# Rotary embedding on one core: a one-row store between the first two loads, and one early row in place of two

## The chip, the cores and the metric

The kernel runs on one core of a Trainium2 chip. The metric is the device time of one execution in microseconds. Before the change the median of three runs is 316.54 us (316.42 to 316.58).

Four engines matter. VectorE (DVE in the profile) does all the arithmetic. ScalarE (ACT) converts between f32 and f16. GpSimd (POOL) issues nearly all transfers; SyncE (SP) issues three and ACT one. The transfers run on 16 DMA engines. TensorE is not used.

## The reference

`x` is [8, 2048, 16, 64] in f32 (batch, position, head, head dimension); `cos` and `sin` are [2048, 32]. Each head vector is cut in two halves of 32, which are rotated against each other by an angle of the position:

```python
cos = cos[None, :, None, :]
sin = sin[None, :, None, :]
out1 = x1 * cos - x2 * sin
out2 = x1 * sin + x2 * cos
return np.concatenate([out1, out2], axis=-1).astype(np.float32)
```

The input and the output are 67.1 MB each, in f32, and each element is read once and written once.

## The kernel before

**Tiles.** A batch has 2048 positions. Partition p of 128 holds J = 16 consecutive positions ("rows"), each of 16 x 64 = 1024 values; a batch is thus 16384 values a partition. The tile `buf` has five slots (`NBUF`), each for one batch, in f16; batch b is in slot b mod 5. Loads from `x` convert f32 to f16 on the way and stores to `out` convert f16 to f32. Both are issued on POOL's queue (lines 71 and 81). A full batch moves 65,536 bytes of f32 a partition on either way.

**Arithmetic.** `rotate` does three VectorE instructions for a range of rows of one batch: a product with the signed sine of the swapped halves into a temporary `v` (line 92), a product with the cosine in place (line 98), and their sum (line 100). ACT prepares the f16 tables `sin_h` and `cos_h` at the start (lines 104 to 106).

**The head rows.** The first JA = 2 rows of batch 0 come another way, so that VectorE can begin early: SyncE loads them as f32 into the tile `head` (line 42), behind the load of `sin` (line 41), and ACT copies them as f16 into slot 0 (line 107). `load(0)` then brings the other 14 rows (`j0 = JA` at line 65). `rotate(0, 0, JA)` works on these two rows alone. At the end of the kernel the same tile is used for the last two rows of batch 7: ACT converts them to f32 (line 134) and SyncE stores them (line 135), while POOL stores rows 0 to 8 and 9 to 13 of that batch.

**Order.** The order of the transfers is written out by hand. The helper `in_ring` (line 51) ties every transfer of POOL to the one before it, so POOL issues them in the order of the program: load 0, load 1, the store of row 0 of batch 0 (line 112), load 2 and 3 as one, load 4, the store of rows 1 to 15 of batch 0, the stores of batches 1 and 2, load 5 and 6, load 7, the stores of 3 and 4, of 5 and 6, and of 7 in its parts. POOL waits in that order too: while it waits for VectorE before a store, the transfers behind it in this list are not issued. Load 5 and 6 waits until the stores of batches 0 and 1 have landed, and load 7 for that of batch 2, since they reuse their slots.

Of the kernel before, what the change touches and what calls it, by code (L numbers as in the profile page):

```python
# [1 line left out]

# [4 lines left out]


@with_exitstack  # L10
def kernel(
    ctx: ExitStack,
    tc: tile.TileContext,
    x: bass.AP,
    cos: bass.AP,
    sin: bass.AP,
    out: bass.AP,
):
    nc = tc.nc
    f16 = mybir.dt.float16  # L20
    f32 = mybir.dt.float32

    B, S, H, D = x.shape
    Dh = D // 2
    P = nc.NUM_PARTITIONS
    J = S // P
    NBUF = 5

    const_pool = ctx.enter_context(tc.tile_pool(name="rope_const", bufs=1))
    io_pool = ctx.enter_context(tc.tile_pool(name="rope_io", bufs=1))  # L30
    tmp_pool = ctx.enter_context(tc.tile_pool(name="rope_tmp", bufs=1))

    JA = 2
    head = const_pool.tile([P, JA, H, D], f32)
    x0 = x[0].rearrange("(p j) h d -> p j (h d)", j=J)
    sin_f = const_pool.tile([P, J, Dh], f32)
    cos_f = const_pool.tile([P, J, Dh], f32)
    cos_h = const_pool.tile([P, J, Dh], f16)
    sin_h = const_pool.tile([P, J, D], f16)
    nc.scalar.dma_start(out=cos_f, in_=cos.rearrange("(p j) d -> p j d", j=J))  # L40
    nc.sync.dma_start(out=sin_f, in_=sin.rearrange("(p j) d -> p j d", j=J))
    nc.sync.dma_start(
        out=head.rearrange("p j h d -> p (j h d)"),
        in_=x0[:, 0:JA, :].rearrange("p j f -> p (j f)"),
    )

    buf = io_pool.tile([P, NBUF, J, H, D], f16)

    ring = []

    def in_ring(dma):
        if ring:
            tc.add_manual_dep(
                dma.ins,
                ring[-1].ins.name,
                mybir.DependencyInfo(mybir.DependencyClass.NoSync, mybir.DependencyReason.DATA),
                reason="order of the ring",
            )
        ring.append(dma)
        return dma  # L60

    def load(b, n=1):
        k = b % NBUF
        if n == 1:
            j0 = JA if b == 0 else 0
            dst = buf[:, k, j0:J, :, :].rearrange("p j h d -> p (j h d)")
            src = x[b].rearrange("(p j) h d -> p j (h d)", j=J)[:, j0:J, :].rearrange("p j f -> p (j f)")
        else:
            dst = buf[:, k : k + n, :, :, :].rearrange("p b j h d -> p b (j h d)")
            src = x[b : b + n].rearrange("b (p j) h d -> p b (j h d)", j=J)  # L70
        in_ring(nc.gpsimd.dma_start(out=dst, in_=src))  # L71

    def store(b, n=1, j0=0, j1=J):
        k = b % NBUF
        if n == 1:
            src = buf[:, k, j0:j1, :, :].rearrange("p j h d -> p (j h d)")
            dst = out[b].rearrange("(p j) h d -> p j (h d)", j=J)[:, j0:j1, :].rearrange("p j f -> p (j f)")
        else:
            src = buf[:, k : k + n, :, :, :].rearrange("p b j h d -> p b (j h d)")
            dst = out[b : b + n].rearrange("b (p j) h d -> p b (j h d)", j=J)  # L80
        return in_ring(nc.gpsimd.dma_start(out=dst, in_=src))  # L81

    def rotate(b, j0=0, j1=J):
        v = tmp_pool.tile([P, J, H, D], f16)
        n = j1 - j0
        js = slice(j0, j1)
        xt = buf[:, b % NBUF, js, :, :]
        shape = [P, n, H, 2, Dh]
        sin_b = sin_h[:, js, :].rearrange("p j (e d) -> p j e d", e=2).unsqueeze(2).to_broadcast(shape)
        cos_b = cos_h[:, js, :].unsqueeze(2).to_broadcast([P, n, 2 * H, Dh])  # L90
        xe = xt.rearrange("p j h (e d) -> p j h e d", e=2)
        nc.vector.tensor_mul(  # L92
            out=v[:, js, :, :].rearrange("p j h (e d) -> p j h e d", e=2),
            in0=xe[:, :, :, ::-1, :],
            in1=sin_b,
        )
        xw = xt.rearrange("p j h (e d) -> p j (h e) d", d=Dh)
        nc.vector.tensor_mul(out=xw, in0=xw, in1=cos_b)  # L98
        xa = xt.rearrange("p j h d -> p (j h d)")
        nc.vector.tensor_add(out=xa, in0=xa, in1=v[:, js, :, :].rearrange("p j h d -> p (j h d)"))  # L100

    load(0)
    load(1)
    nc.scalar.copy(out=sin_h[:, :, Dh:D], in_=sin_f)  # L104
    nc.scalar.mul(out=sin_h[:, :, 0:Dh], in_=sin_f, mul=-1.0)  # L105
    nc.scalar.copy(out=cos_h, in_=cos_f)  # L106
    nc.scalar.copy(  # L107
        out=buf[:, 0, 0:JA, :, :].rearrange("p j h d -> p (j h d)"),
        in_=head.rearrange("p j h d -> p (j h d)"),
    )  # L110
    rotate(0, 0, JA)
    store(0, 1, 0, 1)
    load(2, 2)
    load(4)
    rotate(0, JA, J)
    store(0, 1, 1, J)
    rotate(1)
    store(1)
    rotate(2)
    store(2)  # L120
    load(5, 2)
    load(7)
    rotate(3)
    rotate(4)
    store(3, 2)
    rotate(5)
    rotate(6)
    store(5, 2)
    rotate(7)
    gate = store(7, 1, 0, 9)  # L130
    store(7, 1, 9, J - JA)
    last = buf[:, 7 % NBUF, J - JA : J, :, :].rearrange("p j h d -> p (j h d)")
    dst = out[B - 1].rearrange("(p j) h d -> p j (h d)", j=J)[:, J - JA : J, :].rearrange("p j f -> p (j f)")
    nc.scalar.copy(out=head.rearrange("p j h d -> p (j h d)"), in_=last)  # L134
    end = nc.sync.dma_start(out=dst, in_=head.rearrange("p j h d -> p (j h d)"))
    tc.add_manual_dep(
        end.ins,
        gate.ins.name,
        mybir.DependencyInfo(mybir.DependencyClass.Sync, mybir.DependencyReason.DATA),
        reason="the last rows go out behind this part",  # L140
    )


# [1 line left out]
_INS = ['x', 'cos', 'sin']  # L145
_OUTS = [((8, 2048, 16, 64), 'float32')]


# [23 lines left out]
```

## Time and profile before

| what | value |
|---|---|
| median of three runs | 316.54 us |
| profiled execution, its own time | 316.39 us |
| its span, first to last instruction | 314.6 us |
| outside the span (316.39 - 314.6) | 1.8 us |
| VectorE busy | 209.1 us (66% of the span) |
| ACT busy, POOL busy | 6.7 us, 8.6 us |
| share of the 16 DMA engines taken by POOL's queue (q0) | 98.1% |
| by SP's (q1), by ACT's (q10) | 1.9%, 0.2% |
| HBM read and written | 67.63 MB, 67.11 MB |
| the two head rows, issue to landing | 12.0 us |
| load of the other 14 rows, issue to landing | 22.5 us |
| store of row 0, issue to landing | 25.3 us |

The busy time of an engine says how much it worked, not whether anybody waited for it. The share of the DMA engines is the time that their packets took, over 16 times the span. The trace also holds a record for each packet: its start, its length in time, its queue and its size on the receiving side. Here a packet is what one partition gets or gives in one transfer, and each DMA engine carries 8 of the 128.

### The profile page before, as it was taken

To read this page: it belongs to the slowest core of one execution; us is meant where nothing else is said; L and a number is where in the kernel's file an instruction comes from. 1 tells how busy PE (TensorE), PEld (TensorE's weight loads), DVE (VectorE), ACT (ScalarE), POOL (GpSimd) and SP (SyncE) were. 2 spreads that over 40 slices of the span, in tenths; PEclk is the share of its full clock that TensorE was granted. 3 is DMA by queue.
4 is the path that set the end of the run, shared out by engine and by line. 5 is a ranking of instruction groups with operands and counts; after the bars stand their busy time and mean duration, and the time that the engine had idled before them with its cause. 6 is when DMAs were issued, how large, how long until landed. Compare 5 with 4: busy or idle time off the path is not lost.

```text
span 314.6 us, 114 instructions
## 1 busy us (share of the span) xinstructions
DVE 209.1 (66%) x27; ACT 6.7 (2%) x6; POOL 8.6 (3%) x18
## 2 busy tenths in 40 slices
DVE  0039999992499999999950000899999999910000
ACT  3200000000000000000000000000000000020000
POOL 1020000000000000000010000000000000010000
DMA  7999999999999899999999999999999999999998
GB/s 240 252 242 200 200 267 200 200 267 200 200 200 325 375 500 400 400 400 533 400 200 221 246 200 200 246 221 333 400 508 425 400 400 525 408 400 400 433 425 342
DMA packets 3104, 101.71 MB, mean 323 GB/s; under 512 B 288, under 2 KB 288, under 8 KB 672
## 3 DMA queue, kind: packets, MB, share of 16 engines
q0 software_dynamic: 2528, 99.09, 98.1%
q1 hardware_dynamic: 432, 2.36, 1.9%
q10 hardware_dynamic: 144, 0.26, 0.2%
HBM read 67.63 MB, written 67.11 MB: 428 GB/s over the span
## 4 chain that ended last, share of the span: by engine, by line
DVE 65%; another core or an unknown queue 15%; DMA 7%; ACT 1%; issue 0%; DVEq 0%; ACTq 0%; PEldq 0%
DVE buf L98 22%; DVE v L92 22%; DVE buf L100 22%; DMA buf<-in_x_dram 7%; ACT head L134 1%; DVEq L92 0%; ACTq L134 0%; PEldq L167 0%
## 5 line engine op out<-in xcount | busy, mean ns | idle before, releaser
L92 DVE TENSOR_TENSOR v<-buf,sin_h 128x16384 f16<-128x16384 f16 (+2 forms) x9 | 69.7, 7744 | 66.6 <-DMA buf<-in_x_dram 51.3
L98 DVE TENSOR_TENSOR buf<-buf,cos_h 128x16384 f16<-128x16384 f16 (+2 forms) x9 | 69.7, 7744 | 0.3
L100 DVE TENSOR_TENSOR buf<-buf,v 128x16384 f16<-128x16384 f16 (+2 forms) x9 | 69.7, 7744 | 0.3
L81 POOL DMA_DIRECT2D out_dram<-buf x8 | 4.7, 584 | 219.2 <-DVE buf L100 219.2
L134 ACT CAST head<-buf 128x2048 f32<-128x2048 f16 x1 | 1.9, 1897 | 261.3 <-DVE buf L100 261.3
L71 POOL DMA_DIRECT2D buf<-in_x_dram x6 | 3.7, 628 | 49.7 <-DMA out_dram<-buf 48.9
L107 ACT CAST buf<-head 128x2048 f16<-128x2048 f32 x1 | 1.9, 1897 | 7.1 <-DMA head<-in_x_dram 7.1
L104 ACT ACT_TABLE_LOAD x1 | 1.3, 1283 | 1.2 <-PEq L156 1.2
L104 ACT CAST sin_h<-sin_f 128x512 f16<-128x512 f32 x1 | 0.6, 617 | 2.0 <-DMA sin_f<-in_sin_dram 2.0
L105 ACT ACTIVATE sin_h<-sin_f 128x512 f16<-128x512 f32 x1 | 0.6, 624 | 0.0
L106 ACT CAST cos_h<-cos_f 128x512 f16<-128x512 f32 x1 | 0.6, 601 | 0.0
L156 POOL MEMSET const-float32-0.0<- 128x1 f32 x1 | 0.1, 98 | 0.2 <-issue 0.2
L156 POOL MEMSET const-bfloat16-1.0<- 128x1 bf16 x1 | 0.1, 101 | 0.0
L156 POOL MEMSET const-uint8-127<- 128x1 uint8 x1 | 0.1, 99 | 0.0
L156 POOL MEMSET const-float32-1.0<- 128x1 f32 x1 | 0.1, 98 | 0.0
## 6 DMA issues: line engine op xcount, KB each, us to landing
buf<-in_x_dram POOLq DMA_DIRECT2D x2, 8192.0 KB, 60.3
buf<-in_x_dram POOLq DMA_DIRECT2D x3, 4096.0 KB, 57.4
out_dram<-buf POOLq DMA_DIRECT2D x1, 7680.0 KB, 73.5
out_dram<-buf POOLq DMA_DIRECT2D x1, 4608.0 KB, 28.6
buf<-in_x_dram POOLq DMA_DIRECT2D x1, 3584.0 KB, 22.5
out_dram<-buf POOLq DMA_DIRECT2D x1, 2560.0 KB, 34.1
head<-in_x_dram SPq DMA_DIRECT2D x1, 1024.0 KB, 12.0
out_dram<-head SPq DMA_DIRECT2D x1, 1024.0 KB, 8.4
```

Source lines behind the costliest of these rows:

```text
L71: in_ring(nc.gpsimd.dma_start(out=dst, in_=src))
L81: return in_ring(nc.gpsimd.dma_start(out=dst, in_=src))
L92: nc.vector.tensor_mul(out=v[:, js, :, :].rearrange("p j h (e d) -> p j h e d", e=2), in0=xe[:, :, :, ::-1, :], in1=sin_b,)
L98: nc.vector.tensor_mul(out=xw, in0=xw, in1=cos_b)
L100: nc.vector.tensor_add(out=xa, in0=xa, in1=v[:, js, :, :].rearrange("p j h d -> p (j h d)"))
L104: nc.scalar.copy(out=sin_h[:, :, Dh:D], in_=sin_f)
L105: nc.scalar.mul(out=sin_h[:, :, 0:Dh], in_=sin_f, mul=-1.0)
L106: nc.scalar.copy(out=cos_h, in_=cos_f)
L107: nc.scalar.copy(out=buf[:, 0, 0:JA, :, :].rearrange("p j h d -> p (j h d)"), in_=head.rearrange("p j h d -> p (j h d)"),)
L134: nc.scalar.copy(out=head.rearrange("p j h d -> p (j h d)"), in_=last)
L156: nc = _bacc.Bacc("TRN2", target_bir_lowering=False, num_devices=1)
```

## The change

Two edits. `JA` becomes 1: SyncE loads one row of batch 0 into `head`, ACT copies one row, the first `rotate` works on one row, and `load(0)` brings 15 rows in place of 14. The tile `head` keeps its size of two rows (`JE = 2`), and the end of the kernel still handles two rows through it. And `load(1)` moves from ahead of the first `rotate` to behind the store of row 0, so POOL's order begins: load 0, the store of row 0, load 1, load 2 and 3, load 4.

```diff
-    JA = 2
-    head = const_pool.tile([P, JA, H, D], f32)
+    JA = 1
+    JE = 2
+    head = const_pool.tile([P, JE, H, D], f32)
...
     nc.sync.dma_start(
-        out=head.rearrange("p j h d -> p (j h d)"),
+        out=head[:, 0:JA, :, :].rearrange("p j h d -> p (j h d)"),
         in_=x0[:, 0:JA, :].rearrange("p j f -> p (j f)"),
     )
...
     load(0)
-    load(1)
     nc.scalar.copy(out=sin_h[:, :, Dh:D], in_=sin_f)
...
     nc.scalar.copy(
         out=buf[:, 0, 0:JA, :, :].rearrange("p j h d -> p (j h d)"),
-        in_=head.rearrange("p j h d -> p (j h d)"),
+        in_=head[:, 0:JA, :, :].rearrange("p j h d -> p (j h d)"),
     )
     rotate(0, 0, JA)
     store(0, 1, 0, 1)
+    load(1)
     load(2, 2)
     load(4)
...
-    store(7, 1, 9, J - JA)
-    last = buf[:, 7 % NBUF, J - JA : J, :, :].rearrange("p j h d -> p (j h d)")
-    dst = out[B - 1].rearrange("(p j) h d -> p j (h d)", j=J)[:, J - JA : J, :].rearrange("p j f -> p (j f)")
+    store(7, 1, 9, J - JE)
+    last = buf[:, 7 % NBUF, J - JE : J, :, :].rearrange("p j h d -> p (j h d)")
+    dst = out[B - 1].rearrange("(p j) h d -> p j (h d)", j=J)[:, J - JE : J, :].rearrange("p j f -> p (j f)")
```

## The prediction

> **What bounds the kernel now.** I read the page first: busy shares, the DMA rows, the queues, the HBM line.
>
> ```profile
> DVE 209.1 (66%) x27; ACT 6.7 (2%) x6; POOL 8.6 (3%) x18
> ...
> DMA  7999999999999899999999999999999999999998
> ...
> q0 software_dynamic: 2528, 99.09, 98.1%
> q1 hardware_dynamic: 432, 2.36, 1.9%
> q10 hardware_dynamic: 144, 0.26, 0.2%
> HBM read 67.63 MB, written 67.11 MB: 428 GB/s over the span
> ```
>
> VectorE works two thirds of the span. The DMA row is at 9 in all slices but the first, one in the middle and the last, and the queues' shares add to just over 100%: the 16 DMA engines bound the kernel. The chain of waits names VectorE for 65%, but only because it follows what ended last; VectorE waits for loads three times, and the engines are full meanwhile. The packet records say how full. Added up by the microsecond, packets cover 0.67 of the 16 engines between 2 and 3 us, 1.00 or a little more in every stretch that I added up from 3 to 313 us, 0.44 from 313 to 314 and nothing after. (A packet is recorded as starting some 20 ns before the one ahead of it on its engine has ended.) So the time is: 2 to 3 us until the engines are full, 310 us of packets, 1 us to close. A change can move it by altering the packets' total, or by leaving engines without packets.
>
> Next the start, from the timeline, where both edits lie.
>
> ```profile
> 0.74 0.38 SPq L41 DMA_DIRECT2D sin_f<-in_sin_dram  x1
> 1.17 0.43 SPq L42 DMA_DIRECT2D head<-in_x_dram  x1
> 1.24 1.21 POOL L71 DMA_DIRECT2D buf<-in_x_dram  x2 [0.80 <-PEq L167]
> ...
> 5.51 0.60 ACT L106 CAST cos_h<-cos_f 128x512 f16<-128x512 f32 x1
> 13.22 1.90 ACT L107 CAST buf<-head 128x2048 f16<-128x2048 f32 x1 [7.11 <-DMA head<-in_x_dram]
> 15.15 1.23 DVE L92 TENSOR_TENSOR v<-buf,sin_h 128x2048 f16<-128x2048 f16 x1 [15.15 <-ACT buf L107]
> ...
> 19.19 0.54 POOL L81 DMA_DIRECT2D out_dram<-buf  x1 [16.74 <-DVE buf L100]
> 19.72 1.27 POOL L71 DMA_DIRECT2D buf<-in_x_dram  x2
> 23.87 7.63 DVE L92 TENSOR_TENSOR v<-buf,sin_h 128x14336 f16<-128x14336 f16 x1 [4.98 <-DMA buf<-in_x_dram]
> ```
>
> POOL issues load 0 at 1.24, but the first packet of its queue starts at 5.73. Until then the engines carry sin, cos and the head rows: the head's first packets start between 3.89 and 4.34 us by engine. From 5.73 on a head packet and a packet of load 0 take turns on each engine (2.13 us of load 0, then 0.32 of head, then load 0 again), so the head's last two packets wait for two long ones, and the head lands at 13.2.
>
> **The packets' total does not change.** On an engine a packet occupies, start to start, 0.306 us for 8,192 bytes of f32 (head), 0.153 for 4,096 (the row-0 store), 2.111 for 57,344 (load 0; recorded as 28,672 of f16) and 2.412 for 65,536: 26.8 to 27.2 bytes a nanosecond whatever the size. The head's 8 packets an engine shrink from 8 x 0.306 = 2.45 us to 8 x 0.153 = 1.22, less 1.22; load 0's 8 packets grow by 15/14 to 2.262 each, 8 x 0.151 = 1.21 more. Packet counts are as before. Sum: 0.0 us, within 0.02.
>
> **The row-0 store in another place.** It takes the same 8 packets an engine: after load 0 at about 24 us in place of after load 1 at 42.8. In the records of before, one engine's last load packet ends at 42.83, its eight store packets follow at 0.153 each, and load 2 starts at 44.07, with nothing left open on either side. A boundary of load and store before and one of store and load behind it are there in both orders: 0.0 us.
>
> **The added wait.** In the new order POOL waits for VectorE's row 0 before it issues load 1, and load 2 and 3 and load 4 behind that. Cover: load 0 keeps the engines busy to about 23.8 us. The head, one row, should have all its packets through by 4.34 + 8 x 0.153 = 5.56 us, on the latest engine, before load 0's first packets: it lands near 5.7. ACT is free at 6.1; its copy of 1024 values costs 1.04 us, between the rows 0.617 for 512 and 1.897 for 2048. The three VectorE instructions cost 0.69 each (1.225 for 2048 and 7.626 for 14336 give 0.521 ns a value and 0.16 fixed). 6.1 + 1.04 + 3 x 0.69 + 0.1 for gaps = 9.3; POOL's store at 9.6 (0.3 behind VectorE, as at 19.19 before), load 1 at 10.2, the rest by 12.1. From an issue to its first packet the only row is 1.24 to 5.73, 4.5 us, so the store can be ready at 14.1, and load 1 just behind: 9 us before they are needed. Cost 0; if that cover were gone the engines would stand idle (second rival).
>
> **VectorE later.** Load 0 lands at 23.9 to 24.0 instead of 23.7; VectorE has 15 rows in place of 14 to do from there, 3 x 8.16 = 24.5 in place of 22.9, and so finishes batch 1 at 74.7 in place of 73.0. Before, it then stood idle 10.16 us for load 2 and 3. That cover takes the 1.7 us; store 0 and store 1 are issued that much later, at 49 and 75 us, while loads fill the engines to 102. After 83 us the order of packets and VectorE's waits are as before. The nearest margin is the store of 5 and 6, issued at 250.46 while the packets ahead of it run to 255.7; both hang on the landing of load 5 and 6 and move together.
>
> **Engines without packets at 5.5 us.** This is what remains. The head's packets now run out between 3.89 + 1.22 = 5.11 and 5.56 us by engine, and load 0 is ready when it was. The end is set by the latest engine (at the end they are 0.32 us apart, 313.32 to 313.64), so it counts. There, before, load 0's first packet started at 6.17, with two head packets still open, and the work of load 0 and head was through at 23.70. After: first packet plus 8 x 2.262 = 18.10.
> - Lower bound: load 0 is there when the head ends, 5.56 + 18.10 = 23.66, -0.04 us.
> - Upper bound: not before 6.17, 24.27, +0.57 us.
> - I take 5.8, since 14 of the 16 engines had their first one between 5.73 and 5.96: 23.90, +0.2 us.
>
> The sum on the profiled execution is 316.39 + 0.2 = 316.6. That execution is 0.15 below the median of the three; on the median, 316.7 us, +0.06%, which a measurement of this kernel hardly tells from no change (0.2%, or 0.63 us).
>
> Against a rule: in the trace, a first packet of POOL's queue came 4.5 us after the issue began. The Trainium skill, "DMA: Bandwidth & Descriptors", section "Latency and other measured facts", puts the first byte of a GpSimd transfer at about 1 us. By that, load 0 would be there at about 2.3 us and every head packet would wait for a long one, which is the second rival in full, an estimate of 320 us or more; this case's trace disagrees with the page, 4.5 against 1, and the sum goes by the trace.
>
> **Rivals.**
> 1. *The engines run empty and must fill again (slower).* The very first packet of an engine, 2.0 to 2.2 us, was recorded with up to 0.63 to 0.97 us where those behind it took 0.08. If an engine that has run dry at 5.5 us pays that again on load 0's first packet, 0.55 to 0.9 comes on top of 0.2: 317.2 to 317.7, take 317.4. Against it: consecutive packets overlap in the records, so the next one is fetched while one runs, and load 0's fetch was probably under way before 5.73.
> 2. *The head comes late and the ring runs dry (slower).* If load 0, with nothing issued behind it, is ready earlier than 5.73, each of n head packets left on an engine waits for a long one, 2.26 + 0.15 = 2.41 us. The head then lands at first packet + n x 2.41; the store is issued 3.6 us later (1.04 + 2.07 + 0.4) and ready up to 4.5 us after that. The engines have packets to 23.7, so it decides when the head lands after 23.7 - 8.1 = 15.6: n = 5, load 0's first packet at 4.8 or before. Price: at 4.8, 16.9 + 8.1 - 23.7 = 1.3 us; with all eight left, at 4.3, 23.6 + 8.1 - 23.7 = 8 us: 317.8 to 324.5, near 318 at the edge. Against: on 14 engines five or six head packets had started before load 0's first, and nothing ahead of load 0 on POOL is changed.
> 3. *The row-0 store overlaps the loads (faster).* Placed early, its packets read on-chip memory and write HBM while loads do the reverse; if an engine carried both at once, up to 8 x 0.153 = 1.22 us of the total would go: 315.3. It decides above half of that (0.63 us). Against: at 42.8 to 44.4 the same packets lie between two loads already and overlap nothing beyond the 20 ns.
>
> **How the numbers follow.** Forecast, same within 0.2% (316.5 to 317.1 by the bounds): 0.64. Rival 1: 0.17. Rival 2: 0.09. Rival 3, with whatever else shortens packets: 0.10. That gives faster 0.10, same 0.64, slower 0.26. The range takes in the forecast's bounds, widened by 0.2 below for the runs' own scatter (316.42 to 316.58) and the engines falling into step, and rival 1: 316.3 to 317.7; rivals 2 and 3, 0.19, are left out.
>
> **What would show it.** Right: the head lands 4 to 5 us after its issue in place of 12.0; ACT's copy starts near 6.1, POOL's store near 9.6 and load 1 near 10.2; packets of load 0 run without turns of the head; VectorE's 15-row instructions take 8.16 us and start near 24.0; from 83 us on all instructions stand 0 to 0.6 us later, by the same amount; the DMA row stays at 9. Wrong: a landing of the head after 15 us with a gap in the DMA row near 24 us (rival 2); load 0's first packets recorded near 3 us long (rival 1); later instructions that stand earlier by 0.6 us or more from about 45 us on (rival 3). A drift that builds up after 100 us would mean something that none of these steps contains.

## The result, and the profile after

The changed kernel takes 317.27 us (median of ten runs, 317.05 to 317.73); the kernel before took 316.58 in ten runs beside it (316.41 to 316.78). That is 0.69 us more, a ratio of 1.0025 with a 95% interval of 1.0018 to 1.0033: slower by 0.25%. The interval leaves out no change, but its lower end lies just under the 0.2% that the prediction took for the least that can be told. The profiled pair is 317.28 against 316.39.

The page of the changed kernel, in the lines that answer to those shown of before:

```profile
span 315.5 us, 114 instructions
...
DMA  9899999999999999999999999999999999999997
...
q0 software_dynamic: 2528, 99.35, 98.3%
q1 hardware_dynamic: 432, 1.84, 1.5%
...
HBM read 67.63 MB, written 67.11 MB: 427 GB/s over the span
...
buf<-in_x_dram POOLq DMA_DIRECT2D x1, 3840.0 KB, 23.5
...
head<-in_x_dram SPq DMA_DIRECT2D x1, 512.0 KB, 4.9
```

The 16 DMA engines are as full as before and move the same bytes at 427 in place of 428 GB/s. The head lands 4.9 us after its issue (12.0 before). Load 0 lands 23.5 us after its issue (22.5 before), where the prediction's steps gave 22.7 to 22.8.

The timeline of the changed kernel (start, length, instruction, and in brackets the idle time ahead of it):

```profile
1.24 0.67 POOL L72 DMA_DIRECT2D buf<-in_x_dram  x1 [0.80 <-PEq L168]
...
6.08 1.04 ACT L107 CAST buf<-head 128x1024 f16<-128x1024 f32 x1
7.16 0.69 DVE L93 TENSOR_TENSOR v<-buf,sin_h 128x1024 f16<-128x1024 f16 x1 [7.16 <-ACT buf L107]
...
9.62 0.53 POOL L82 DMA_DIRECT2D out_dram<-buf  x1 [7.71 <-DVE buf L101]
10.14 1.81 POOL L72 DMA_DIRECT2D buf<-in_x_dram  x3
24.86 8.16 DVE L93 TENSOR_TENSOR v<-buf,sin_h 128x15360 f16<-128x15360 f16 x1 [15.56 <-DMA buf<-in_x_dram]
...
84.05 8.69 DVE L93 TENSOR_TENSOR v<-buf,sin_h 128x16384 f16<-128x16384 f16 x1 [8.46 <-DMA buf<-in_x_dram]
...
141.38 0.71 POOL L72 DMA_DIRECT2D buf<-in_x_dram  x1 [30.36 <-DMA out_dram<-buf]
...
306.24 0.35 SPq L136 DMA_DIRECT2D out_dram<-head  x1
```

and of the kernel before, where the same three late points stand:

```profile
83.16 8.69 DVE L92 TENSOR_TENSOR v<-buf,sin_h 128x16384 f16<-128x16384 f16 x1 [10.16 <-DMA buf<-in_x_dram]
...
140.48 0.71 POOL L71 DMA_DIRECT2D buf<-in_x_dram  x1 [30.35 <-DMA out_dram<-buf]
...
305.34 0.35 SPq L135 DMA_DIRECT2D out_dram<-head  x1
```

ACT, VectorE and POOL do their first work at the predicted moments (6.1, 7.2, 9.6, 10.1). The loss is there at 84 us, 0.89 us, and is still 0.90 at 141 and at 306: all of it arises before 84 us and is then carried along. A waiting engine sees only the last of the 16 DMA engines: the head lands on them between 5.23 and 6.06 us, and ACT starts at 6.08. So the packet records must say how the 16 stand. Three numbers from them are used below: by how much the head's packets are longer than the shortest of their size, added up and divided by 16 ("head excess"); how much the last load packets ahead of the row-0 store are longer than the others of their size, as a mean of the 16 engines ("boundary"); and the last landing of the kernel, as a mean of the 16 and by how much the latest is behind that mean ("lag").

All packet times from here on are on the clock of the timeline. Those of the prediction and of the expectations stand 0.24 us later than that clock: the prediction's first packets of load 0 at 5.73 to 6.17 are at 5.49 to 5.93. The DMA view of the kernel before, from 3 to 6 us, confirms it, since it counts all 16 of them as started ahead of 6.00:

```profile
q0 software_dynamic: 16, 0.46, 71.0%
```

Differences between packets are not touched by this. A time from an issue, which was read on the timeline, to a packet is: the prediction's 4.5 us from load 0's issue to its first packet is 4.25.

| us | head excess | latest first packet of load 0, behind the mean | boundary | last landing, mean | lag | median of the runs |
|---|---|---|---|---|---|---|
| before | 0.03 | 0.31 | 0.19 | 313.56 | 0.19 | 316.58 |
| after | 0.18 | 0.57 | 0.41 | 313.93 | 0.72 | 317.27 |

The 0.90 us of the profiled pair is 0.37 in the mean engine and 0.53 in lag. No engine stood empty between the head and load 0: load 0's first packets start at 4.89 on the first engine and at 5.75 on the last, each within 10 ns of the end of the head. But on some engines the head took longer: 20 of its 128 packets took more than 0.18 us, one of them 0.62, where the rest took 0.16. In the mean, 0.17 of the 0.37 is there when load 0 lands, its boundary set aside, and 0.2 comes at the boundary. On the engine that ends last, the boundary counts for more: its last load packet ahead of the store is 0.57 us longer in the changed kernel, and 0.10 in the kernel before.

### The profile page after: what moved, and what is told of

Its sections match the earlier page's. It is cut to its first block, busy times and chain, and to the rows that moved or that the text cites. A ratio compares the mean times of both kernels' runs of the same rounds, so it can differ in the third digit from the quotient of the medians.

```text
span 315.5 us, 114 instructions
## 1 busy us (share of the span) xinstructions
DVE 209.1 (66%) x27; ACT 5.9 (2%) x6; POOL 8.6 (3%) x18
## 4 chain that ended last, share of the span: by engine, by line
DVE 66%; another core or an unknown queue 14%; DMA 7%; ACT 1%; issue 0%; DVEq 0%; ACTq 0%; PEldq 0%
DVE v L93 22%; DVE buf L99 22%; DVE buf L101 22%; DMA buf<-in_x_dram 7%; ACT head L135 1%; DVEq L93 0%; ACTq L135 0%; PEldq L168 0%
## 5 line engine op out<-in xcount | busy, mean ns | idle before, releaser
L107 ACT CAST buf<-head 128x1024 f16<-128x1024 f32 x1 | 1.0, 1045 | 0.1
## 6 DMA issues: line engine op xcount, KB each, us to landing
buf<-in_x_dram POOLq DMA_DIRECT2D x1, 3840.0 KB, 23.5
```

The source lines that it names most:

```text
L107: nc.scalar.copy(out=buf[:, 0, 0:JA, :, :].rearrange("p j h d -> p (j h d)"), in_=head[:, 0:JA, :, :].rearrange("p j h d -> p (j h d)"),)
```

## The experiments

All medians below are beside the kernel before, run on the same chip at the same time, whose median was 316.57 us in both of the larger sets.

**One edit at a time.** The first kernel takes the one-row head alone, the second the new order alone.

```diff
 # first: from the changed kernel
     load(0)
+    load(1)
...
     store(0, 1, 0, 1)
-    load(1)
 # second: from the kernel before
     load(0)
-    load(1)
...
     store(0, 1, 0, 1)
+    load(1)
```

> One early row, but load 1 ahead of the first rotation as before. Theory A (two sizes at the start: the engines begin load 0 unevenly behind the one-row head, the latest 0.7 us behind the mean at the end in place of 0.2; and the last load packets ahead of the row-0 store are longer, 0.37 us lost a mean engine in place of 0.21): it keeps the first part and loses the second, +0.3 to +0.5 us on the kernel before, 316.9 to 317.1. Theory B (the order alone costs it): no change, 316.5 to 316.7.

> Two early rows as before, but load 1 behind the row-0 store. Theory A: only the longer boundary, +0.1 to +0.2 us, 316.7 to 316.8. Theory B: all of the change, +0.6 to +0.8 us, 317.2 to 317.4. The third theory, of the prediction's second rival (up to 4.5 us from issue to first packet): the store is issued at 19.2 and would be ready at 23.7, where load 0 ends, so a gap of 0 to 1 us would stand in the packets at 24 us.

The first took 317.27 us (317.05 to 317.39), a ratio of 1.0019 (1.0011 to 1.0028): all of the change's time, without the new order, and more than theory A gave (316.9 to 317.1). Theory B falls. In its profiled execution (317.05) the head excess is 0.12, load 0's latest first packet is 0.53 behind the mean, the boundary 0.25, the last landing 313.82 with a lag of 0.59. Its timeline has the loss at the same places, a little smaller:

```profile
6.10 1.04 ACT L108 CAST buf<-head 128x1024 f16<-128x1024 f32 x1 [0.20 <-DMA head<-in_x_dram]
...
24.30 8.16 DVE L93 TENSOR_TENSOR v<-buf,sin_h 128x15360 f16<-128x15360 f16 x1 [14.98 <-DMA buf<-in_x_dram]
...
83.81 8.69 DVE L93 TENSOR_TENSOR v<-buf,sin_h 128x16384 f16<-128x16384 f16 x1 [8.79 <-DMA buf<-in_x_dram]
...
306.01 0.35 SPq L136 DMA_DIRECT2D out_dram<-head  x1
```

The second, of twelve executions, had seven at 316.33 to 316.84 and five at 317.99 to 319.05. Its median of 316.67 therefore says little, and its ratio of 1.0024 (1.0004 to 1.0043) mixes two kinds. The profiled one was of the first kind (316.48): head excess 0.03, boundary 0.29, lag 0.13, and no gap in the packets at 24 us. So the new order alone need not cost anything, but sometimes costs 1.4 to 2.5 us; that is taken up below.

**Without the row-0 store.** Batch 0 is stored whole.

```diff
     rotate(0, 0, JA)
-    store(0, 1, 0, 1)
...
-    store(0, 1, 1, J)
+    store(0)
```

> The kernel before without the store of row 0 between the loads: batch 0 is stored whole. Theory A: the boundary's 0.21 us goes, 316.3 to 316.4. Theory B, by which the boundary costs nothing: 316.5 to 316.7.

It took 317.04 us (316.87 to 317.46), ratio 1.0013 (1.0005 to 1.0022): slower, where both theories had no change or a gain. The cost of the boundary does not vanish with the row-0 store, it moves to the next boundary. The last packets of load 4, at 100 us ahead of the first store that is left, are 0.52 us longer in the mean; in the kernel before, with the row-0 store ahead of it, that boundary had no packet longer than 25 ns over its size. So the small store is a cheap place to pay for the first turn from loading to storing: 0.19 us in place of 0.52, in one profile of each.

**Small packets without the change.** The kernel before, with the two head rows as two transfers:

```diff
-    nc.sync.dma_start(
-        out=head.rearrange("p j h d -> p (j h d)"),
-        in_=x0[:, 0:JA, :].rearrange("p j f -> p (j f)"),
-    )
+    for j in range(JA):
+        nc.sync.dma_start(
+            out=head[:, j : j + 1, :, :].rearrange("p j h d -> p (j h d)"),
+            in_=x0[:, j : j + 1, :].rearrange("p j f -> p (j f)"),
+        )
```

> The kernel before, the two head rows loaded as two transfers of one row, so that SyncE's packets are 4,096 bytes as in the changed kernel, twice as many. Theory A with small packets as the reason of the uneven start: head packets longer than 0.16 us, the engines further apart at load 0, +0.3 to +0.5 us, 316.9 to 317.1. If the uneven start has another reason (that load 0 is alone in POOL's queue, or chance): 316.5 to 316.7.

317.22 us (317.03 to 317.43), ratio 1.0019 (1.0011 to 1.0028). Same rows, same order, load 0 of 14 rows with load 1 behind it, and the loss is there, again a little more than theory A gave: head excess 0.26 over 16 packets an engine (some 0.1 of it from taking turns with load 0), load 0's latest first packet 0.60 behind the mean, lag 0.66. So neither the 15-row load nor a lone load 0 is the reason; head packets of 4,096 bytes are.

**Is it the size, or where the rows lie?** In `x` the head row of one partition is 65,536 bytes from that of the next. This kernel has one early row and the old order, but SyncE fetches 128 rows that follow each other. Row 0 of each partition then holds another position's data; sizes and counts stay:

```diff
-        in_=x0[:, 0:JA, :].rearrange("p j f -> p (j f)"),
+        in_=x[0].rearrange("s h d -> s (h d)")[0:P, :],
```

> One early row and the old order (as the first experiment), but SyncE fetches 128 rows that lie one behind the other in HBM, partition p the position p, in place of every sixteenth row. Row 0 of each partition is thus computed from another position; sizes and counts are as before. If the head packets' extra time (0.12 to 0.18 us a mean engine, up to 0.5 us in one packet) comes from the distance of the rows in HBM, it goes: excess under 0.05 us, engines within 0.3 us of the mean at the end, 316.5 to 316.7. If it comes from packets of 4,096 bytes as such, nothing changes: 317.1 to 317.3.

316.66 us (316.53 to 317.12), ratio 1.0004 (0.9995 to 1.0013). Every one of the 128 head packets took 0.159 us, the head excess is 0.00, load 0's latest first packet 0.26 behind the mean, the lag 0.28. The timeline follows: 

```profile
5.75 1.04 ACT L108 CAST buf<-head 128x1024 f16<-128x1024 f32 x1
...
23.88 8.16 DVE L93 TENSOR_TENSOR v<-buf,sin_h 128x15360 f16<-128x15360 f16 x1 [14.92 <-DMA buf<-in_x_dram]
...
83.42 8.69 DVE L93 TENSOR_TENSOR v<-buf,sin_h 128x16384 f16<-128x16384 f16 x1 [8.81 <-DMA buf<-in_x_dram]
```

The one-row head would be harmless if its rows lay together; it is small packets from rows far apart that stall. With 8,192 bytes from rows just as far apart (the kernel before) the head excess is 0.03, what a turn with load 0 costs. The Trainium skill, "DMA: Bandwidth & Descriptors", section "Latency and other measured facts", reports a loss from row pitches of large powers of two: copies between HBM tensors, in tiles of 16 KiB a partition, ran at 207 GB/s with a pitch of 512 KiB, 164 with 2 MiB and 103 with 4 MiB, against 214 with the 4 MiB padded by 4 KiB. It lists no pitch as small as the 64 KiB of this case. Whether this is the same effect is not shown: no run here has a second pitch, so a power of two is not told from any other distance.

**Is it the place in SyncE's queue?** One early row, old order, head ahead of sine:

```diff
-    nc.sync.dma_start(out=sin_f, in_=sin.rearrange("(p j) d -> p j d", j=J))
     nc.sync.dma_start(
         out=head[:, 0:JA, :, :].rearrange("p j h d -> p (j h d)"),
         in_=x0[:, 0:JA, :].rearrange("p j f -> p (j f)"),
     )
+    nc.sync.dma_start(out=sin_f, in_=sin.rearrange("(p j) d -> p j d", j=J))
```

> One early row and the old order, but SyncE loads the head row ahead of the sine table. If the head packets are slow because they are the second transfer in SyncE's ring, they now take 0.16 us, and the engines are within 0.3 us of the mean at the end: 316.5 to 316.7. If packets of 4,096 bytes are slow as such at this point: 317.0 to 317.4, engines as uneven as in the changed kernel (latest 0.6 to 0.7 us behind the mean).

317.11 us (316.90 to 317.61), ratio 1.0019 (1.0010 to 1.0028). The loss stays; load 0's latest first packet is 0.56 behind the mean, the lag 0.41 and the last landing's mean 314.00. The head excess is even 0.71, but here the head also shares the engines with the cosine load, and the two reasons are not told apart. It is not the order of SyncE's two loads that makes the loss.

**The cover of the new wait.** The changed kernel, with the row-0 store held back:

```diff
-    nc.scalar.copy(out=cos_h, in_=cos_f)
+    for _ in range(31):
+        nc.scalar.copy(out=cos_h, in_=cos_f)
```

> The changed kernel with 30 more copies of the cosine table on ACT (0.53 us each), all ahead of VectorE's second instruction for row 0, so that the row-0 store is issued at about 24.8 us in place of 9.6, after load 0 has ended (23.8 to 24.4). The second rival's wait: the engines stand without packets from 24 us until the first store packet. If an issue takes up to 3.9 us to its first packet (load 0: issued at 1.24, there at 5.13 at the latest): 4 to 5 us slower than the changed kernel, 321 to 322. If it takes about 1 us: 2 us slower, 319.

One execution, 324.14 us, outside both expectations. The copies took 0.65 us each, so the store was issued at 28.17 and not at 24.8. Its timeline:

```profile
6.97 19.44 ACT L107 CAST cos_h<-cos_f 128x512 f16<-128x512 f32 x30
...
28.17 0.53 POOL L82 DMA_DIRECT2D out_dram<-buf  x1 [26.27 <-DVE buf L101]
28.70 1.81 POOL L72 DMA_DIRECT2D buf<-in_x_dram  x3
```

and its DMA view from 20 to 32 us, 40 slices of 0.3 us (packets count where they start):

```profile
DMA  0099940000000000000000000000001999999500
...
out_dram<-buf POOLq DMA_DIRECT2D x1, 512.0 KB, 3.5
```

Load 0's last packets start by 21.5 and end by 23.8; nothing but their end marks starts from there until the store. The store's first packet is at 29.27, 1.10 us after the issue. This is the second rival as a fact: with the wait uncovered, the engines stand empty, here for some 6 us on the mean engine (23.3 to 29.3), and the time follows: 6.9 us over the changed kernel. Later the last packets of load 4 are 0.99 us longer in the mean, as if the row-0 store, which came to empty engines and not behind running loads, had not paid for the first boundary; against that, the engines restarted together, and the lag is 0.19 in place of 0.72.

**What lies behind the five times near 318 to 319 us of the new order with two rows?** First the guard: ACT copies the two rows one by one, and VectorE rotates only row 0 ahead of the store.

```diff
-    nc.scalar.copy(
-        out=buf[:, 0, 0:JA, :, :].rearrange("p j h d -> p (j h d)"),
-        in_=head.rearrange("p j h d -> p (j h d)"),
-    )
-    rotate(0, 0, JA)
+    for j in range(JA):
+        nc.scalar.copy(
+            out=buf[:, 0, j : j + 1, :, :].rearrange("p j h d -> p (j h d)"),
+            in_=head[:, j : j + 1, :, :].rearrange("p j h d -> p (j h d)"),
+        )
+    rotate(0, 0, 1)
...
-    rotate(0, JA, J)
+    rotate(0, 1, J)
```

> New order with two early rows (as the second experiment), but ACT copies the rows one by one and VectorE rotates row 0 alone before the store; row 1 goes with the other 14. The store is issued near 16.8 us in place of 19.2. The second experiment had 7 times in 12 about 316.5 and 5 times 318.0 to 319.1. If those five are a ring run dry because the head landed one long packet (2.4 us) later, the 2.4 us gained here cover it: all executions 316.4 to 317.0. If they have another reason, some stay above 318.

All eleven executions were at 316.36 to 316.67, median 316.46, ratio 0.9997 (0.9988 to 1.0007). So the new order as such costs nothing that can be measured, and with a store issued earlier, here at 16.7 us, no time near 318 came up. Whether those times were a ring run dry is another matter. Three more executions of the kernel with two rows and the new order:

> The second experiment again, one look, to see what its executions near 318 to 319 us are made of. If the ring ran dry: the head lands at 18 us (four packets left on one engine) in place of 13.2, the store is issued near 24, its first packet starts 1.34 us later (as in the experiment with the late store), the engines stand empty for 1 to 2 us and the time is 318 to 319. If the head lands by 15.6: no gap, 316.3 to 316.9. A time of 318 or more without a gap would speak for another reason.

> As the run before it: either the head lands by 15.6 us, no gap at 24 us and 316.3 to 316.9; or it lands near 18, a gap of 1 to 2 us and 318 to 319.

> As the two runs before it: either the head lands by 15.6 us, no gap at 24 us and 316.3 to 316.9; or it lands near 18, a gap of 1 to 2 us and 318 to 319.

They took 318.05, 316.53 and 316.61 us. The first is one of those near 318:

```profile
15.27 1.90 ACT L106 CAST buf<-head 128x2048 f16<-128x2048 f32 x1 [9.22 <-DMA head<-in_x_dram]
...
21.26 0.53 POOL L81 DMA_DIRECT2D out_dram<-buf  x1 [19.35 <-DVE buf L100]
...
83.33 8.69 DVE L92 TENSOR_TENSOR v<-buf,sin_h 128x16384 f16<-128x16384 f16 x1 [10.18 <-DMA buf<-in_x_dram]
...
142.14 0.71 POOL L71 DMA_DIRECT2D buf<-in_x_dram  x1 [31.84 <-DMA out_dram<-buf]
```

the second is one of the others:

```profile
12.96 1.90 ACT L106 CAST buf<-head 128x2048 f16<-128x2048 f32 x1 [7.16 <-DMA head<-in_x_dram]
...
18.95 0.53 POOL L81 DMA_DIRECT2D out_dram<-buf  x1 [17.03 <-DVE buf L100]
...
83.30 8.69 DVE L92 TENSOR_TENSOR v<-buf,sin_h 128x16384 f16<-128x16384 f16 x1 [10.07 <-DMA buf<-in_x_dram]
...
140.64 0.71 POOL L71 DMA_DIRECT2D buf<-in_x_dram  x1 [30.37 <-DMA out_dram<-buf]
```

and so is the third, though its head and its store are as late as in the first:

```profile
15.17 1.90 ACT L106 CAST buf<-head 128x2048 f16<-128x2048 f32 x1 [9.28 <-DMA head<-in_x_dram]
...
21.15 0.53 POOL L81 DMA_DIRECT2D out_dram<-buf  x1 [19.24 <-DVE buf L100]
...
140.70 0.71 POOL L71 DMA_DIRECT2D buf<-in_x_dram  x1 [30.52 <-DMA out_dram<-buf]
```

In the first of them the head did land one long packet later than in the second (15.3 against 13.0) and the store was issued 2.3 us later, but there was no gap: packets cover the engines fully from 22 to 28 us, and at 83 us the two stand together. The 1.5 us arise between 83 and 142. The packet records of the first have the place: no load packet ahead of the row-0 store is longer than usual, but the last packets of load 4 are, by 0.82 us in the mean and 1.55 on the worst engine. My explanation, a ring run dry, was wrong: this execution paid the first boundary at load 4, as the kernel with the late store and the kernel without the row-0 store did. But a late store is not enough for that. In the third execution, too, no load packet ahead of the row-0 store is longer, and yet the last packets of load 4 are only 0.12 us longer; the packets of the row-0 store itself are, by 0.32 in the mean (0.23 in the first). What decides between the two, what happens in an engine at the first turn from loads to stores, and why it costs less ahead of a small store that was queued early, no run here shows. The five times of the second experiment near 318 and 319 have no profile.

## Why the prediction was wrong where it was

The time lies in the range of 316.3 to 317.7, but not within the forecast's own bounds of 316.5 to 317.1: no change was forecast as likeliest, and the kernel became slower by 0.69 us. The range reaches this far only because it takes in rival 1, whose mechanism did not occur; that the time lies in it is luck. Two terms of the sum failed, the length of the head's packets and the boundary.

- *The packets' total does not change.* Right for the bytes and for the usual length of each size. The sum of 0.0 was wrong, since single packets took longer: the mean engine ends 0.37 us later.
- *The head should have its packets through by 5.56 us on the latest engine, at 0.153 us each.* This is the first step that failed. The 0.153 came from the row-0 store, which writes to HBM with full queues; the head reads rows 64 KiB apart at the start, and took up to 0.62 for a packet. On the prediction's clock it was through at 5.99 on the latest engine, 0.43 later (5.32 and 5.75 on the timeline's). The mean engine lost 0.12 to 0.18 us; the sum had none.
- *Engines without packets at 5.5 us.* Wrong. There was no empty time on any engine: load 0 was there whenever the head ended, from 4.89 on. Its "lower bound" was the right case for when load 0 is ready, yet the first packet of load 0 on the latest engine came nearer the upper bound (5.99, on the prediction's clock, between 5.56 and 6.17), because the head ran long. Put into the prediction's own sum, 5.99 gives 24.09, +0.4 us in place of the +0.2 of the forecast.
- *The latest engine sets the end.* Right, and more so than I thought: the engines' distance at load 0 is still there 290 us later. The lag is 0.72 in place of 0.19, more than half of the loss in the profiled pair.
- *The row-0 store in another place, 0.0 us.* Right as a price of the move: the kernel with both rows loaded, the new order and one row rotated has a ratio of 0.9997 (0.9988 to 1.0007). Wrong in its reason, that nothing is lost at that boundary, and this is the second step that failed: 0.19 to 0.41 us are lost in a mean engine, in all nine profiles in which that store stood queued in time, and the prediction considered only the packets behind the load's last one.
- *What the two terms come to.* On the engine that ends last, the start of its last load packet ahead of that store gives what had gone wrong until then, and the packet's length the boundary. Against the profile of the kernel before, the changed kernel has 0.39 us of late start and 0.47 of boundary (0.57 in place of 0.10), together 0.86 of its 0.89. One row in the old order has 0.43 and 0.22, of 0.66; with rows that follow each other it is 0.01 and 0.25, of 0.26. So the place of the rows explains the late start, but not the boundary, and why that varies is open. The profiled execution of the kernel before is also one of its fastest, 0.19 below its median; in the medians the kernel with rows that follow each other is only 0.09 slower.
- *The added wait is covered.* Right, with a wider margin: 1.10 us from issue to first packet in the kernel with the late store, not up to 4.5. The Trainium skill's figure of about 1 us ("DMA: Bandwidth & Descriptors", section "Latency and other measured facts"), which I set aside for the row of the first issue, holds for this one.
- *VectorE later by 1.7 us, hidden.* Right: 84.05 is 83.16 plus the 0.89 of the engines and no more.
- *Rival 1* (0.55 to 0.9 us where engines must fill again) has the size but not the cause: load 0's first packets took 2.28 us, as all of their size. *Rival 2* was made to happen, and does not happen in the changed kernel. *Rival 3*, faster, did not come.

The edits are linked: with two early rows, the new order is at times 1.4 to 2.5 us slower. That did not occur with one early row, in ten executions, nor with a store issued at 16.7 us, in eleven; the one early row costs 0.7 us in the median.

## What to carry to other kernels

In a kernel that is bound by DMA engines, count not only bytes but how evenly the 16 engines start: each carries its own 8 of the 128 packets of a transfer, and as long as the queues stay full the distance stays. The latest engine was 0.71 us behind the mean when load 0 landed, and 0.72 when the kernel ended 290 us later. Price a small transfer from records of the same direction, size and distance in memory; a store's packet time does not hold for a load of far-apart rows. When a term is bounded by "the engine may be empty", bound "the packet may be longer" beside it.

## What was not expected of the hardware

- Loads of 4,096 bytes a partition from rows 65,536 bytes apart stalled at the start, up to 0.62 us for a packet of 0.16; from rows that follow each other none did, and with 8,192 bytes, in the kernel before, none did by more than the turn with load 0.
- The first turn from loads to stores lengthens the last load packet on each engine: 0.19 to 0.41 us ahead of a small store that was queued early, 0.52 to 0.99 at the next boundary in three profiles where that store was missing or late. In a fourth, with the store just as late, it was 0.12 there. In the kernel before, the same boundary at load 4 cost nothing.
- From the issue of a GpSimd store to its first packet on empty engines it was 1.10 us, in one run; for the first load of the changed kernel, issued at 1.24 us, it is at most 3.65, since its first packet, at 4.89, came right behind the head.
